# Receptance and value products of the second token group between the preparation steps of the first, and the second recurrence ahead of the first outputs

## The chip, the core and the metric

The kernel runs on one core of a Trainium2 chip. TensorE (PE in the rows) does the matrix products, VectorE (DVE) and ScalarE (ACT) the elementwise work, GpSimd (POOL) a smaller part of it, and SyncE (SP) issues the transfers. The metric is the time of one execution on the device in microseconds. The kernel before takes 2268.82 us (median of 3 runs, 2268.51 to 2272.32).

## The reference

One inference step of a decoder with two layers: layer 0 mixes tokens with an RWKV-7 recurrence, layer 1 with dilated attention, and each is followed by a gated feed-forward block. There are 512 prompt tokens and 8 x 4 = 32 sample tokens, 1024 features, 16 heads of 64. Only layer 0's mixing is touched. Cut to what matters:

```python
def rwkv7_time_mix(xn, x_last, S0, mu, w_rkv, ...):
    xs = xn[:, :, None, :] + xx[:, :, None, :] * mu
    rkv = jnp.einsum('btnc,ncd->btnd', xs[:, :, :3], w_rkv)
    r, k, v = rkv[:, :, 0], rkv[:, :, 1], rkv[:, :, 2]
    xw, xa, xg = xs[:, :, 3], xs[:, :, 4], xs[:, :, 5]
    w_log = -jax.nn.softplus(-(w0 + jnp.tanh(xw @ w1) @ w2)) - 0.5
    decay = jnp.exp(-jnp.exp(w_log.astype(F32)))
    a = jax.nn.sigmoid(a0 + (xa @ a1) @ a2)
    g = jax.nn.sigmoid(xg @ g1) @ g2
    ...
    y, S_T = wkv7_scan(rh, heads(decay), kh, vh, -kk, kk * ah, S0.astype(F32))
    ...
    bonus = jnp.sum(rh * kh * r_k, axis=-1, keepdims=True) * vh
    y = y + bonus.reshape(B, T, D)
    out = (y * g) @ w_o
```

The scan is `S = S * w_t + (S a_t) b_t + v_t k_t`, `y = S r_t` for each token and head.

## The kernel before

All products of the layer are float32 results of three passes over split operands (`mm3`, L98 to L100: high by high, high by low, low by high), where `split` (L74, L75) takes the high part on ScalarE and the low part on VectorE or GpSimd. The 544 token columns go in two groups, g0 with 288 (256 prompt and the 32 sample ones) and g1 with 256. A product of one kind (receptance i=0, key i=1, value i=2) for one group is 8 blocks m of 128 outputs, each 8 x 3 matmuls: 192 matmuls 128x288 or 128x256. `proj_gemm` runs it, loads its weights in transfers of 256 KB and splits them. Its inputs come from `mix`: 8 calls of `mix_block`, each one multiply-add on VectorE (`mix_t`, L306), one copy on ScalarE and one subtraction on VectorE or GpSimd. Tiles `mx` feed the three large products, `mxe` (one buffer) the low-rank ones of `lora1`.

The recurrence runs in chunks of 64 tokens. For each group, `prep(g)` calls `unit_prep` for 8 units of two heads: low-rank products L414 to L416, head sums L135, transposes of v (L458), elementwise work that ends in the tiles `AR`, `BK` and `BE`, and in a second half (after the `yield`) the bonus L485, the transposes of `BE` (L493) and the products of `BK` by `AR` (L498), which VectorE masks into `G`. The second half of a unit is issued after the first half of the next. `inverses` then solves the triangular systems of all chunks: copies of `G` into `X` (L515), a transpose (L518), 62 small VectorE operations (L523, L526), two transposes back (L529, L530), copies, and small products on TensorE (L539, L549). `chain`, which the text calls the scan, walks the chunks (from L570). `samples(hb)` does the sample tokens of half the heads (state loads and transposes L640, L648; products L653 to L706). `y_norm` takes mean and variance of the outputs (a power `y_var` on GpSimd, then four multiplications of `yt` there), and `y_out` applies gate and bonus and stores (`lg_hi`, `lg_lo`: split gate weights). `states` writes the final states. After the layer come `w_o`, the feed-forward blocks and attention.

The code is written as one stream, and the framework orders each engine's instructions from it; `Stream` (`c.slow`) limits how far the units of a preparation run ahead. Before, that gives: key and receptance for both groups with the low-rank products beside them; value for g0 with `prep(0)` in between, and value for g1 drawn into the same stretch; the rest of `prep(0)`; `inverses(0)`; scan(0); `samples(0)`, `prep(1)` and `samples(1)`; `inverses(1)`; scan(1) with `outputs(0)`; `states` and `outputs(1)`.

The lines of the driver that set this:

```python
        for m, _ in enumerate(proj_gemm(c, 2, mv, stage, groups=(0,))):
            next(p0, None)
        ...
        run(p0)
        inverses(c, st[0]["G"], sa)
        run(proj_gemm(c, 2, mv, stage, groups=(1,)))
        scan(0)
        ysm.append(samples(c, 0, smp[0], sp))
        run(prep(1))
        ysm.append(samples(c, 1, smp[1], sp))
        inverses(c, st[1]["G"], sa)
        outputs(0)
        scan(1)
```

Of the kernel before, what the change touches and what calls it, by code (L numbers as in the profile page):

```python
# [396 lines left out]
def unit_prep(c, g, m, b, up, un, G, UV):  # L397
# [11 lines left out]
    split(c, lhi, llo, lw, nc.vector, nc)  # L409
# [46 lines left out]
    ps = c.pp()  # L456
# [4 lines left out]
    BK = up.tile([128, 4, 2, 64], F, name="BK", bufs=c.ub)  # L461
# [4 lines left out]
    nc.vector.tensor_copy(c.dc[:, m, :, g], dp[:, :, 64])  # L466
# [38 lines left out]
def inverses(c, G, sp):  # L505
# [3 lines left out]
    nc = c.nc  # L509
    first, second = [[slice(side_of(par)[1].start + 32 * b, side_of(par)[1].start + 32 * b + 32) for par in range(2)]  # L510
# [3 lines left out]
    for r, view in blk:  # L514
        nc.scalar.activation(X[r], view, AF.Copy)  # L515
# [15 lines left out]
    for r, view in blk:  # L531
        nc.scalar.activation(view, X[r], AF.Copy)
    Z = sp.tile([128, 32, 32], F, name="XL", bufs=1)
    for n0 in (0, 16):
# [6 lines left out]
        for par in range(2):  # L541
            r1 = second[par]
            nc.scalar.activation(Z[r1, n0:n0 + 16, :], ps[par][r1, :].rearrange("p (n t) -> p n t", t=32), AF.Copy)
    for n0 in (0, 16):
# [6 lines left out]
        for par in range(2):  # L551
            r0 = first[par]
            nc.scalar.activation(G[r0, par, n0:n0 + 16, 96:128], ps[par][r0, :].rearrange("p (n t) -> p n t", t=32), AF.Copy)
# [181 lines left out]
def y_out(c, g, jj, yt, ys, yo):  # L735
# [13 lines left out]
    for par in range(2):  # L749
# [7 lines left out]
        split(c, lhi, llo, lg, nc.vector, nc)  # L757
# [25 lines left out]
def rwkv(c):  # L783
    nc, tc, a = c.nc, c.tc, c.a
    with ExitStack() as rx:
        ps = rx.enter_context(c.pool("ps", space=PSUM))
# [8 lines left out]
        c.pp = lambda: ps.tile([128, 512], F, name="pp", bufs=2)  # L795
# [26 lines left out]
        def scan(g):  # L822
            st[g]["yt"] = [sa.tile([128, 512], F, name=f"yt{x}", bufs=1) for x in range(4)]
            chain(c, g, st[g]["units"], st[g]["G"], st[g]["UV"], st[g]["yt"], sa)

        def outputs(g):
            y_norm(c, st[g]["yt"] + (ysm if g == 0 else []), yo)
# [15 lines left out]
        c.mm = lambda: pm.tile([128, 512], F, name="mm", bufs=6)  # L843
        stage = rp.enter_context(c.pool("stage", side="right"))
# [4 lines left out]
        with ExitStack() as ex:  # L849
# [15 lines left out]
            def side():  # L865
                for g in range(2):
                    mr.append(mix(c, 0, g, m1, "mx", bufs=2))
                    yield
                yield from lora1(c, lp, late, lambda i, g: mix(c, i, g, late, "mxe", bufs=1))
            sd = side()  # L870
            for _ in proj_gemm(c, 1, mk, stage):
                next(sd, None)
            for m, _ in enumerate(proj_gemm(c, 0, mr, stage)):
                next(sd, None)
                if m < 2:
                    mv.append(mix(c, 2, m, (ma, mb)[m], "mx", bufs=1))
            run(sd)
        rq.close()
        us = rx.enter_context(c.pool("us"))
        u0 = rx.enter_context(c.pool("u0"))  # L880
        up = rx.enter_context(c.pool("up"))
        c.ub = 1
        p0 = prep(0)
        for m, _ in enumerate(proj_gemm(c, 2, mv, stage, groups=(0,))):
            next(p0, None)
        px.close()
        ra.close()
        pm = py.enter_context(c.pool("ps_mm2", space=PSUM))
        c.mm = lambda: pm.tile([128, 512], F, name="mm", bufs=2)
        c.cw = lambda: pm.tile([128, 512], F, name="cw", bufs=1)  # L890
        c.cp = c.iv = lambda: pm.tile([128, 512], F, name="cp", bufs=3)
        run(p0)
        sa = rx.enter_context(c.pool("sa"))
        c.W = sa.tile([128, 512], F, name="W")
# [3 lines left out]
        inverses(c, st[0]["G"], sa)  # L898
        run(proj_gemm(c, 2, mv, stage, groups=(1,)))
        scan(0)  # L900
        py.close()
        rb.close()
        rp.close()
        pq = rx.enter_context(c.pool("ps_pp", space=PSUM))
        c.sm = lambda: pq.tile([128, 512], F, name="sm", bufs=1)
        c.cw = lambda: pq.tile([128, 512], F, name="cw", bufs=1)
        c.cp = c.iv = lambda: pq.tile([128, 512], F, name="cp", bufs=4)
# [738 lines left out]
```

## Time and profile before

| what | us |
|---|---|
| median of 3 runs | 2268.82 |
| lowest and highest | 2268.51, 2272.32 |
| the profiled execution | 2266.54 |
| its span, first to last instruction | 2264.80 |
| of the span, up to the end of the recurrent layer's recurrence | 604.20 |
| of the span, `w_o`, feed-forward, attention, feed-forward | 1660.60 |
| TensorE busy over the span | 2078.8 (92%) |
| mean granted TensorE clock, share of full speed | 0.937 |

Read the page first for the 40 slices: TensorE is full in all slices but some of the first eleven. Then cut these first 604 us into stages by the first instruction of each, and read busy time per engine and granted clock of every stage; the rows for that stand below.

### The profile page before, as it was taken

The numbers are of one execution on the slowest core, as the hardware profiler recorded it, in microseconds if no ns is written. First come the engines' busy times: TensorE is split into PE (matmuls) and PEld (weight loads), VectorE is DVE, ScalarE is ACT, GpSimd is POOL, SyncE is SP. The second block draws the span as 40 slices with busy tenths as digits, with TensorE's granted clock in tenths as the row PEclk, the third lists the DMA queues.
The fourth block names the chain that finished last, engine by engine and source line by source line (L and its number), as shares of the span: only waits on it lengthen the run. The fifth ranks groups of instructions, "written<-read, shape, count | busy, mean of one in ns | idle before, by whom it ended". The sixth has DMA issues, their size and how long they took to land. (4 is left out here: it accounts for less than half of the span.)

```text
span 2264.8 us, 48471 instructions
## 1 busy us (share of the span) xinstructions
PE 2078.8 (92%) x19286; PEld 1946.8 (86%) x19286; DVE 1167.0 (52%) x2454; ACT 896.4 (40%) x1847; POOL 552.1 (24%) x714
## 2 busy tenths in 40 slices
PE   7999647767599999999999999999999999999998
PEld 6998436546499999999989888888899799999998
DVE  7767565674574344325454454455444664444323
ACT  6555333323254444324333333333334454444323
POOL 5635513541232222102111111111111132222101
PEclk9999658668699999999999999999999999999999
DMA  5236201312653233335544444444444443232333
GB/s 162 91 119 195 74 19 32 74 22 67 175 148 91 83 90 93 93 100 168 138 134 133 120 128 127 119 126 139 123 133 122 133 132 93 85 94 85 88 89 108
DMA packets 435453, 245.96 MB, mean 109 GB/s; under 512 B 43194, under 2 KB 426330, under 8 KB 435098
## 3 DMA queue, kind: packets, MB, share of 16 engines
q1 hardware_dynamic: 435226, 242.86, 37.7%
q8 instruction: 152, 2.49, 0.4%
q14 instruction: 75, 0.61, 0.1%
HBM read 198.55 MB, written 30.85 MB: 101 GB/s over the span
## 5 line engine op out<-in xcount | busy, mean ns | idle before, releaser
L99 PE MATMUL mm<-xn,w_hi 128*128 128x256 f32 (+1 forms) x2688 | 788.0, 294 | 1.4 <-DVE xn L75 0.8
L98 PE MATMUL mm<-xn,w_hi 128*128 128x256 f32 (+1 forms) x2688 | 784.3, 293 | 3.6 <-ACT xn L984 3.6
L100 PE MATMUL mm<-xn,w_lo 128*128 128x256 f32 (+1 forms) x2688 | 780.1, 291 | 0.0
L75 DVE TENSOR_TENSOR w_lo<-w_raw,w_hi 128x512 fp32r<-128x512 f32 (+2 forms) x559 | 421.3, 756 | 568.2 <-ACT w_hi L74 557.2
L74 ACT ACTIVATE w_hi<-w_raw 128x512 fp32r<-128x512 f32 (+2 forms) x559 | 345.8, 620 | 542.1 <-PE mm L99 492.8
L98 PEld LDWEIGHTS mm<-xn,w_hi 128*128 128x128 f32 x2688 | 509.3, 190 | 10.1 <-ACT xn L984 4.2
L99 PEld LDWEIGHTS mm<-xn,w_hi 128*128 128x128 f32 x2688 | 509.6, 190 | 6.0 <-issue 2.8
L100 PEld LDWEIGHTS mm<-xn,w_lo 128*128 128x128 f32 x2688 | 508.8, 189 | 3.1 <-issue 3.0
L98 PE MATMUL mm<-act,w_hi 128*128 128x288 f32 (+1 forms) x704 | 200.4, 288 | 1.6 <-ACT y_out L1017 1.6
L99 PE MATMUL mm<-act,w_hi 128*128 128x288 f32 (+1 forms) x704 | 199.8, 288 | 0.0
L100 PE MATMUL mm<-act,w_lo 128*128 128x256 f32 (+1 forms) x704 | 198.7, 288 | 0.0
L1171 POOL TENSOR_TENSOR qk_raw<-qk_raw,rope 128x1088 f32<-128x1088 f32 x24 | 86.3, 3596 | 419.4 <-DMA qk_sw<-qk_raw 419.4
L98 PEld LDWEIGHTS mm<-act,w_hi 128*128 128x128 f32 x704 | 131.8, 189 | 1.7 <-ACT y_out L1017 1.7
L99 PEld LDWEIGHTS mm<-act,w_hi 128*128 128x128 f32 x704 | 131.6, 188 | 0.0
L100 PEld LDWEIGHTS mm<-act,w_lo 128*128 128x128 f32 x704 | 130.6, 188 | 0.0
L147 POOL TENSOR_TENSOR acc<-acc,sq_t 128x288 f32<-128x288 f32 (+1 forms) x56 | 46.7, 834 | 327.4 <-ACT sq_t L146 327.1
L98 PE MATMUL mm<-mx,w_hi 128*128 128x288 f32 (+1 forms) x384 | 112.1, 295 | 0.0
L100 PE MATMUL mm<-mx,w_lo 128*128 128x256 f32 (+1 forms) x384 | 110.3, 292 | 1.5 <-DVE w_lo L75 1.5
L99 PE MATMUL mm<-mx,w_hi 128*128 128x256 f32 (+1 forms) x384 | 111.2, 293 | 0.0
L1256 ACT ACTIVATE scores<-scores,sm_m 128x512 f32<-128x512 f32 (+3 forms) x80 | 50.4, 631 | 70.9 <-DVE sm_m L1255 68.9
L100 PEld LDWEIGHTS mm<-mx,w_lo 128*128 128x128 f32 x384 | 72.5, 190 | 2.4 <-DVE w_lo L75 2.1
L98 PEld LDWEIGHTS mm<-mx,w_hi 128*128 128x128 f32 x384 | 72.9, 191 | 1.1 <-ACT p_out L373 0.2
(360 smaller groups left out, 3287.0 us busy)
## 6 DMA issues: line engine op xcount, KB each, us to landing
w_raw<-ffn_w_up SPq DMA_DIRECT2D x176, 256.0 KB
w_raw<-attn_w_in SPq DMA_DIRECT2D x144, 256.0 KB
w_raw<-ffn_w_down SPq DMA_DIRECT2D x90, 256.0 KB
w_raw<-rwkv_w_rkv SPq DMA_DIRECT2D x64, 256.0 KB
qk_sw<-qk_raw SPq DMA_DIRECT2D x96, 136.0 KB
cache_k<-cache_k_w SPq DMA_DIRECT2D x96, 128.0 KB
cache_v<-cache_v_w SPq DMA_DIRECT2D x96, 128.0 KB
w_raw<-rwkv_w_o SPq DMA_DIRECT2D x32, 256.0 KB
```

The source lines that it names most:

```text
L74: (nc or c.nc).scalar.activation(out_hi, src, AF.Copy)
L75: lo_engine.tensor_tensor(out_lo, src, out_hi.bitcast(F), OP.subtract)
L98: nc.tensor.matmul(ps, hi, xhi(i), start=first and i == 0, stop=False)
L99: nc.tensor.matmul(ps, hi, xlo(i), start=False, stop=False)
L100: nc.tensor.matmul(ps, lo, xhi(i), start=False, stop=last and i == len(w) - 1)
L147: nc.gpsimd.tensor_tensor(acc, acc, t[:, :n], OP.add)
L1171: nc.gpsimd.tensor_tensor(raw, raw, c.rope[:, 0:1].to_broadcast([128, 2, NT]), OP.mult)
L1256: nc.scalar.activation(s[:, :w], s[:, :w], AF.Exp, scale=0.125, bias=m[:, 1:2], accum_out=m[:, 2:3])
```

## The change

- `mix`: all low parts are subtracted on GpSimd, not on VectorE and GpSimd in turn. `l_lo` and `lg_lo` go from VectorE to GpSimd, the copy into `dc` from VectorE to ScalarE.
- Receptance and value of g0 are computed ahead of `prep(0)`. Receptance and value of g1 (384 matmuls 128x256) come in two blocks m per unit of `prep(0)`; the receptance weights are loaded and split a second time for it.
- `BK` has two buffers in `prep(0)`, `pp` six PSUM buffers there and three later (two before); `yt` has two buffers, and `X` and its like lie in a pool of their own.
- The copies of `inverses` go to ScalarE and VectorE in turn, those into `X` in two halves.
- After scan(0) is issued, `prep(1)` goes one unit ahead, `samples(0)` stands before its next four units and `samples(1)` before the last; then `y_norm` of g0, `inverses(1)`, scan(1), `outputs(0)`, `states`, `y_norm` of g1 and `outputs(1)`.

```diff
@@ mix
-        mix_block(c, i, g, k, mx, c.nc.gpsimd if k % 2 else c.nc.vector)
+        mix_block(c, i, g, k, mx, c.nc.gpsimd)
@@ unit_prep
-    split(c, lhi, llo, lw, nc.vector, nc)
+    split(c, lhi, llo, lw, nc.gpsimd, nc)
...
-    BK = up.tile([128, 4, 2, 64], F, name="BK", bufs=c.ub)
+    BK = up.tile([128, 4, 2, 64], F, name="BK", bufs=c.ubk)
...
-    nc.vector.tensor_copy(c.dc[:, m, :, g], dp[:, :, 64])
+    nc.scalar.activation(c.dc[:, m, :, g], dp[:, :, 64], AF.Copy)
@@ inverses
+    def move(i):
+        return nc.vector.tensor_copy if i % 2 else lambda out, src: nc.scalar.activation(out, src, AF.Copy)
...
-    for r, view in blk:
-        nc.scalar.activation(X[r], view, AF.Copy)
+    by = lambda t: t.rearrange("p (c j) t -> p c j t", j=8)
+    for lo in (0, 4):
+        for i, (r, view) in enumerate(blk):
+            move(i)(by(X[r])[:, :, lo:lo + 4], by(view)[:, :, lo:lo + 4])
...
@@ y_out
-        split(c, lhi, llo, lg, nc.vector, nc)
+        split(c, lhi, llo, lg, nc.gpsimd, nc)
@@ rwkv
-            st[g]["yt"] = [sa.tile([128, 512], F, name=f"yt{x}", bufs=1) for x in range(4)]
+            st[g]["yt"] = [sa.tile([128, 512], F, name=f"yt{x}", bufs=2) for x in range(4)]
...
-            for m, _ in enumerate(proj_gemm(c, 0, mr, stage)):
+            for m, _ in enumerate(proj_gemm(c, 0, mr, stage, groups=(0,))):
                 next(sd, None)
...
+            for m, _ in enumerate(proj_gemm(c, 2, mv, stage, groups=(0,))):
+                if m == 1:
+                    mv.append(mix(c, 2, 1, mb, "mx", bufs=1))
...
-        c.cp = c.iv = lambda: pm.tile([128, 512], F, name="cp", bufs=3)
+        c.pp = c.iv = lambda: pm.tile([128, 512], F, name="pp", bufs=6)
+        p0 = prep(0)
+        rest = proj_gemm(c, 0, mr, stage, groups=(1,))
+        for m in range(9):
+            next(p0, None)
+            for _ in range(2):
+                next(rest, None)
+            if m == 4:
+                run(rest)
+                ra.close()
+                rest = proj_gemm(c, 2, mv, stage, groups=(1,))
         run(p0)
+        inverses(c, st[0]["G"], si)
+        run(rest)
...
-        ysm.append(samples(c, 0, smp[0], sp))
-        run(prep(1))
-        ysm.append(samples(c, 1, smp[1], sp))
-        inverses(c, st[1]["G"], sa)
+        scan(0)
+        p1 = prep(1)
+        next(p1)
+        for hb in range(2):
+            ysm.append(samples(c, hb, smp[hb], sp))
+            for _ in range(4):
+                next(p1)
+        run(p1)
+        y_norm(c, st[0]["yt"] + ysm, yo)
+        inverses(c, st[1]["G"], si)
+        scan(1)
         outputs(0)
-        scan(1)
         for hb in range(2):
             states(hb)
+        y_norm(c, st[1]["yt"], yo)
         outputs(1)
```

What the framework makes of it, at three places. On TensorE, one of the later units of `prep(0)` (`hwa` by `l_hi`: the low-rank products; `hr_e`: head sums; `in`: v), before:

```order
L498 MATMUL pp<-AR,BK 128x128 x8
L414 MATMUL pp<-hwa,l_hi 128x288
L415 MATMUL pp<-hwa,l_hi 128x288
L416 MATMUL pp<-hwa,l_lo 128x288
...
L135 MATMUL pp<-ca,hr_e 128x128 x3
L458 MATMUL pp<-ca,in_2926 64x128 x4
L485 MATMUL pp<-pb,ca 128x288
L493 MATMUL pp<-ca,BE 128x128 x4
L498 MATMUL pp<-AR,BK 128x128 x8
```

and an early unit of the changed kernel (`mx_1641`: mixed input of the receptance product of g1):

```order
L416 MATMUL pp<-hwa,l_lo 128x288
L100 MATMUL mm<-mx_1641,w_lo 128x256
L98 MATMUL mm<-mx_1641,w_hi 128x256
...
L135 MATMUL pp<-ca,hr_e 128x128 x3
L458 MATMUL pp<-ca,in_2659 64x128 x4
L98 MATMUL mm<-mx_1641,w_hi 128x256
...
L485 MATMUL pp<-pb,ca 128x288
L493 MATMUL pp<-ca,BE 128x128 x4
L498 MATMUL pp<-AR,BK 128x128 x8
```

Where a unit's own products followed each other, 28 matmuls of g1 now stand between L416 and L135, and 14 between L458 and L485; there are some 48 per unit, and none is left after the last unit's L498.

On GpSimd in the mixing stretch (`mxe`: inputs of the low-rank products; `rk`: powers for the norms of the keys), before:

```order
L383 TENSOR_TENSOR rk_81<-rs_k,mhalf 128x6
L75 TENSOR_TENSOR mxe_863<-mix_t,mxe_863 128x288 x3
L383 TENSOR_TENSOR rk_81<-rs_k,mhalf 128x4
L75 TENSOR_TENSOR mxe_863<-mix_t,mxe_863 128x288
L383 TENSOR_TENSOR rk_82<-rs_k,mhalf 128x6
```

and in the changed kernel:

```order
L75 TENSOR_TENSOR mxe_744<-mix_t,mxe_744 128x288 x8
L383 TENSOR_TENSOR rk_77<-rs_k,mhalf 128x6
L383 TENSOR_TENSOR rk_77<-rs_k,mhalf 128x4
L75 TENSOR_TENSOR mxe_889<-mix_t,mxe_889 128x288 x3
L383 TENSOR_TENSOR rk_78<-rs_k,mhalf 128x6
```

Of a mix of 8 blocks GpSimd took 4 and now takes 8, between the same powers.

On GpSimd at the end of `prep(1)` (`BK`, `BE`: the last unit; `y_var`: the power of the first group's `y_norm`), before:

```order
L59 TENSOR_TENSOR BK<-th_5072,di 128x4x64
L59 TENSOR_TENSOR BK<-tk,di 128x4x64
...
L59 TENSOR_TENSOR BE<-BK,dc 128x512
...
L59 TENSOR_TENSOR y_var<-y_var,mhalf 128x40
L59 TENSOR_TENSOR um<-Vs,cb 128x512
```

and in the changed kernel:

```order
L59 TENSOR_TENSOR BK<-th_5387,di 128x4x64
L59 TENSOR_TENSOR BK<-tk,di 128x4x64
L59 TENSOR_TENSOR y_var<-y_var,mhalf 128x40
L59 TENSOR_TENSOR BE<-BK,dc 128x512
L59 TENSOR_TENSOR um<-Vs,cb 128x512
```

The power now stands ahead of the last unit's `BE`, which L493 of that unit reads; L498 stands behind L493 on TensorE.

## Rows read from the trace of the kernel before

**Rows 1.** Stages: from:to us, length, busy of PE, PEld, DVE, ACT, POOL, clock, DMA, GB/s

```profile
32.60:165.90 133.30, 128.94 (x1001) 127.44 (x1000) 101.09 (x189) 75.72 (x188) 68.48 (x75) 0.97 0.38 118
165.90:233.60 67.70, 66.39 (x496) 61.70 (x494) 49.17 (x89) 36.63 (x81) 34.90 (x62) 1.00 0.63 185
233.60:294.30 60.70, 38.80 (x169) 28.99 (x167) 32.48 (x70) 18.67 (x40) 31.38 (x69) 0.58 0.25 69
294.30:338.40 44.10, 15.55 (x275) 13.28 (x275) 29.27 (x68) 13.46 (x21) 4.53 (x9) 0.50 0.01 4
338.40:370.60 32.20, 25.29 (x609) 23.63 (x608) 16.92 (x26) 8.41 (x16) 6.32 (x6) 0.89 0.01 2
370.60:465.10 94.50, 74.14 (x423) 58.54 (x420) 56.96 (x103) 37.00 (x77) 52.14 (x79) 0.75 0.28 66
465.10:518.20 53.10, 33.37 (x369) 24.46 (x369) 39.26 (x86) 14.41 (x21) 19.27 (x13) 0.57 0.13 22
518.20:563.00 44.80, 37.41 (x701) 32.30 (x699) 25.79 (x54) 10.15 (x23) 6.39 (x6) 0.91 0.22 64
563.00:604.20 41.20, 13.65 (x54) 9.42 (x49) 17.55 (x33) 7.24 (x16) 10.82 (x5) 0.56 0.60 175
604.20:2264.80 1660.60, 1626.95 (x15129) 1553.37 (x15129) 778.94 (x1693) 654.24 (x1319) 306.15 (x372) 0.99 0.41 115
```

**Rows 2.** TensorE's timeline: start, duration, line, tiles, of matmuls one behind the other

```profile
188.28 0.30 PE L99 MATMUL mm<-mx,w_hi 128*128 128x288 f32 x1
188.41 0.29 PE L100 MATMUL mm<-mx,w_lo 128*128 128x288 f32 x1
...
207.57 0.28 PE L99 MATMUL mm<-mx,w_hi 128*128 128x256 f32 x1
207.69 0.28 PE L100 MATMUL mm<-mx,w_lo 128*128 128x256 f32 x1
```

**Rows 3.** Groups by form, 32 to 168 us: total us, mean ns, idle before and releaser

```profile
L383 POOL TENSOR_TENSOR rk<-rs_k,mhalf 128x6 f32<-128x6 f32 x8 | 12.0, 1506 | 7.4 <-DVE rs_k L382 5.7 <-DMA w_raw<-rwkv_w_rkv 1.7
L75 POOL TENSOR_TENSOR mxe<-mix_t,mxe 128x288 fp32r<-128x288 f32 x12 | 10.7, 896 | 6.7 <-ACT mxe L74 6.7
L383 POOL TENSOR_TENSOR rk<-rs_k,mhalf 128x4 f32<-128x4 f32 x8 | 9.3, 1164 | 3.8 <-DVE rs_k L382 3.8
...
L75 DVE TENSOR_TENSOR w_lo<-w_raw,w_hi 128x512 fp32r<-128x512 f32 x32 | 23.0, 718 | 25.0 <-ACT w_hi L74 25.0
L75 DVE TENSOR_TENSOR mxe<-mix_t,mxe 128x288 fp32r<-128x288 f32 x12 | 6.0, 498 | 0.1
```

**Rows 4.** GpSimd's waits, 160 to 300 us: total us, times, longest

```profile
POOL BK L59 <- PE pp L498: 38.8, 7, 8.4
```

**Rows 5.** VectorE and TensorE timelines, first solve: its transposes, first product behind it

```profile
296.89 1.95 DVE L518 STREAM_TRANSPOSE XL<-X 128x1024 f32<-128x1024 f32 x1
...
323.13 1.91 DVE L529 STREAM_TRANSPOSE XT<-XL 128x1024 f32<-128x1024 f32 x1
...
325.10 0.32 PE L539 MATMUL cp<-XT,G 32*32 32x32 f32 x4 [22.80 <-DVE XT L529]
```

**Rows 6.** VectorE's timeline, second solve: the same two transposes

```profile
467.87 1.97 DVE L518 STREAM_TRANSPOSE XL<-X 128x1024 f32<-128x1024 f32 x1 [2.73 <-ACT X L515]
...
504.00 1.91 DVE L529 STREAM_TRANSPOSE XT<-XL 128x1024 f32<-128x1024 f32 x1
```

**Rows 7.** Timelines of SyncE and GpSimd: state loads of the samples, power of y_norm

```profile
372.93 2.90 SPq L640 DMA_DIRECT2D st<-state_rwkv_wkv  x4
...
489.08 7.78 POOL L59 TENSOR_TENSOR y_var<-y_var,mhalf 128x40 f32<-128x40 f32 x1 [5.63 <-DVE y_var L59]
```

**Rows 8.** Timelines of GpSimd and VectorE in the outputs of g1

```profile
572.79 5.39 POOL L59 TENSOR_TENSOR yt<-yt,y_var 128x512 f32<-128x512 f32 x4
...
573.33 5.40 DVE L75 TENSOR_TENSOR w_lo<-w_raw,w_hi 128x512 fp32r<-128x512 f32 x4 [6.19 <-ACT w_hi L74]
...
588.60 0.29 DVE L59 TENSOR_TENSOR lg_lo<-lg_raw,lg_hi 128x128 fp32r<-128x128 f32 x1 [0.51 <-ACT lg_hi L59]
```

More of the change, by code (lines that the diff above doesn't have):

```diff
@@ L530, in inverses @@
     nc.vector.transpose(X.rearrange("p n t -> p t n"), flat)
-    for r, view in blk:
-        nc.scalar.activation(view, X[r], AF.Copy)
+    for i, (r, view) in enumerate(blk):
+        move(i)(view, X[r])
     Z = sp.tile([128, 32, 32], F, name="XL", bufs=1)
@@ L542, in inverses @@
             r1 = second[par]
-            nc.scalar.activation(Z[r1, n0:n0 + 16, :], ps[par][r1, :].rearrange("p (n t) -> p n t", t=32), AF.Copy)
+            move(par)(Z[r1, n0:n0 + 16, :], ps[par][r1, :].rearrange("p (n t) -> p n t", t=32))
     for n0 in (0, 16):
@@ L552, in inverses @@
             r0 = first[par]
[L553 removed]
+            move(par)(G[r0, par, n0:n0 + 16, 96:128], ps[par][r0, :].rearrange("p (n t) -> p n t", t=32))
 def chain(c, g, units, G, UV, yt, sp):
@@ L843, in rwkv @@
         c.mm = lambda: pm.tile([128, 512], F, name="mm", bufs=6)
+        c.pp = lambda: pm.tile([128, 512], F, name="pp", bufs=2)
         stage = rp.enter_context(c.pool("stage", side="right"))
@@ L865, in side @@
             def side():
-                for g in range(2):
-                    mr.append(mix(c, 0, g, m1, "mx", bufs=2))
-                    yield
+                mr.append(mix(c, 0, 0, m1, "mx", bufs=2))
+                yield
                 yield from lora1(c, lp, late, lambda i, g: mix(c, i, g, late, "mxe", bufs=1))
             sd = side()
-            for _ in proj_gemm(c, 1, mk, stage):
+            for m, _ in enumerate(proj_gemm(c, 1, mk, stage)):
                 next(sd, None)
-            for m, _ in enumerate(proj_gemm(c, 0, mr, stage)):
+                if m == 5:
+                    mv.append(mix(c, 2, 0, m1, "mx", bufs=2))
@@ L879, in rwkv @@
         us = rx.enter_context(c.pool("us"))
         u0 = rx.enter_context(c.pool("u0"))
[L881 to L887, printed above, removed]
+        si = rx.enter_context(c.pool("si"))
+        ux = ExitStack()
+        up = ux.enter_context(c.pool("up"))
+        c.ub, c.ubk = 1, 2
         pm = py.enter_context(c.pool("ps_mm2", space=PSUM))
@@ L893, in rwkv @@
+        run(p0)
+        inverses(c, st[0]["G"], si)
+        run(rest)
+        py.close()
+        rb.close()
+        rp.close()
+        ux.close()
+        pq = rx.enter_context(c.pool("ps_pp", space=PSUM))
+        c.sm = lambda: pq.tile([128, 512], F, name="sm", bufs=1)
+        c.cw = lambda: pq.tile([128, 512], F, name="cw", bufs=1)
+        c.cp = lambda: pq.tile([128, 512], F, name="cp", bufs=3)
+        c.pp = c.iv = lambda: pq.tile([128, 512], F, name="pp", bufs=3)
         sa = rx.enter_context(c.pool("sa"))
+        up = rx.enter_context(c.pool("up1"))
@@ L894, in rwkv @@
+        c.ubk = 1
         c.W = sa.tile([128, 512], F, name="W")
```

19 lines of the change are left out of this document (3 added, 16 removed).

## The prediction

> **What bounds the kernel now.** I began with the 40 slices of the page and then cut the span into stages [rows 1]. The last stage, 1660.6 us from 604.20 on, has TensorE busy for 1626.95 us at a clock of 0.99, and the change leaves TensorE's work there alone: it counts as zero. Everything is decided in the first 604 us, where three kinds of stages alternate. While large products run, TensorE is the bound: busy 128.94 of 133.30 us and 66.39 of 67.70. Once the value products have run out, four of the eight units of `prep(0)` take 60.70 us at a granted clock of 0.58, with TensorE busy 38.80, VectorE 32.48 and GpSimd 31.38: no engine is full, and it is a chain from engine to engine that sets the pace. In the two solves (44.10 and 53.10 us at 0.50 and 0.57) the same holds, with VectorE's string of small operations as the chain. So the ground to win is the time in which TensorE idles or runs at half clock: 60.7, 44.1, 94.5, 53.1 and 41.2 us. The change moves products from stages where TensorE is full into the first of them.
>
> **Up to the first unit of `prep(0)`.** One matmul follows the next at 0.12 us with 256 columns and at 0.13 with 288 [rows 2]. Ahead of 165.9, receptance of g1 goes out (192 x 0.12 = 23.0) and value of g0 comes in (192 x 0.13 = 25.0): +1.9, so 168 at the least. To that comes the move of the low parts. By the last low-rank mix, 64 blocks (48 low-rank, 8 receptance, 8 value) lie on GpSimd, 32 more than before. On GpSimd one takes 896 ns, on VectorE 498 [rows 3]: GpSimd gains 32 x 0.896 = 28.7 us and VectorE loses 15.9. The powers of the key norms stay on GpSimd, 12.0 + 9.3 = 21.3 us, in the same queue. GpSimd then has 64 x 0.896 + 21.3 = 78.6 us of work, and with 0.56 us (6.7 / 12) of waiting for ScalarE before each block some 114, in a stage of 133.3. It fits, but no longer with room: the low-rank tile `mxe` has one buffer, so every delay goes on to the next mix, and TensorE has in front of it only what is left of receptance and value for g0. If the difference of 12.8 us all came through, the first unit would start at 181; if none, at 168. I take half: 174.
>
> The Trainium skill speaks against this move (GPSIMD Engine Reference, section 4.1, Engine selection): elementwise work with two inputs belongs on VectorE, since GpSimd is about twice as slow. The trace agrees nearly, 896 against 498 ns being 1.8 times; by the page's factor of 2 the difference would be an estimated 15.9 us and the upper end 184 in place of 181.
>
> **`prep(0)`.** Before, it lasted from 165.9 to 294.3. After, each unit carries 48 matmuls of g1, 5.8 us. What a unit needs of TensorE on its own: in the dense stretch 496 matmuls ran, 384 of them large, and these take 48 us of 67.7; the 112 others are those of four units, so 19.7 / 4 = 4.9 us each. TensorE's floor is thus 10.7 us per unit. GpSimd's is 31.38 / 4 = 7.8, and 8.3 with the two low parts that it now gets. The chain's is what ran before without large products: 60.70 / 4 = 15.2 us per unit. What sat in the chain was `BK`, which waited for the unit before's L498, 38.8 us in 7 waits, 5.5 us each [rows 4]; its second buffer takes that wait away. What is late next is `BE` with its one buffer, and TensorE's queue, in which a unit's L135, L485 and L493 now stand behind 14 to 28 matmuls (1.7 to 3.4 us). I expect 12 us per unit, nearer to TensorE's floor, since the gap between the two, 4.5 us, is less than the wait of 5.5 that goes; the clock should stay up, as in the dense stretch at 1.00. Seven units at 12 and 15 for the last with its second half: 174 + 84 + 15 = 273, **21 us less** than 294.3. The ends: 168 + 7 x 10.7 + 12 = 255 (39 less) and 181 + 7 x 15.2 + 15 = 302 (8 more). The second load of the receptance weights (16 transfers and splits) is hidden: DMA is busy at 0.25 and VectorE at 32.48 of 60.7 there.
>
> **`inverses(0)`.** The copies into `X` took from 294.3 to 296.9 on ScalarE alone; on two engines half, -1.3. The solve between the transposes, 296.89 to 325.04, stays but for some small operations of the preparation in between, -0.7. From L539 at 325.10 [rows 5] to the scan at 338.4 products and copies take turns for 13.3 us; the copies on two engines give -3 (0 to -5). Sum **-5** (-2 to -7).
>
> **scan(0)** took 32.20 us with TensorE busy 25.29. The first unit of `prep(1)` (4.9) and the first half of `samples(0)`, taken as much again, come into its queue: 10 us less what fits in the 6.9 idle ones. **+7** (3 to 11).
>
> **From scan(0) to scan(1)**, before 94.5 + 53.1 us. The unit that has gone into scan(0): an eighth of 94.5, -12. The rest of `samples(1)`, which ran beside the second solve from 465.1 until its power at 489.1, 24 us, now stands ahead of it; half beside the units, +12 (0 to 24). The power takes 7.78 us [rows 7] and stands on GpSimd ahead of the last unit's `BE`; behind it wait L493 and L498, `G`, `X` and the solve: +7.8. The 16 state loads of `samples(1)` are issued in a row into two buffers at 2.90 / 4 us each [rows 7], so 11.6 in all; TensorE's 16 transposes wait in order with the later units behind them: +8 (0 to 11.6). Against that, the second solve is free of the samples' work: between its transposes 467.87 to 505.91 [rows 6], 38.0 us, against 28.1 in the first [rows 5]: -9.9. The copies into `X` -1.4, those after the solve -2.5. Sum **+2** (-18 to +18).
>
> **scan(1) with outputs(0)**, 44.80 us against 32.20 for the scan alone. The outputs are still needed in between, but the scan goes first: I take 3 of the 12.6, **-3** (-8 to +2). **`states`, `y_norm` and outputs of g1**, 41.20 us: eight `lg_lo` go from VectorE, 0.29 each, to GpSimd at some 0.5, behind the multiplications of `yt` (5.39 us) [rows 8]: **+3** (0 to 8).
>
> **The sum.** -21 - 5 + 7 + 2 - 3 + 3 = -17 on the profiled execution's 2266.5, which is 2249.5. That execution lies 2.3 us under the median of 2268.8, so 2252 for the median.
>
> **The rivals.** First, **the units keep their 15.2 us**. The wait on `BK` may only have hidden another, `BE`'s or that for TensorE's queue, so that the chain is as long as before: 174 + 7 x 15.2 + 15 = 295, 22 us later than in the sum, which gives 2274; with the mixes late as well (181) 2281. It decides from about 15 us per unit on. For it speaks that 60.7 us held no full engine, and that at the half clock the 48 matmuls would take 11.6 in place of 5.8 us; against it the 5.5 us that go. What would feed it: beside the four `yt` multiplications, four `w_lo` took 5.40 us on VectorE, 1.35 each [rows 8], against 0.718 [rows 3], so the two engines hold each other up where they work at once. The Trainium skill gives the reason (SBUF — State Buffer, section SBUF: two separate sides): VectorE with two inputs from there and GpSimd share one pair of ports, which one of them holds for a whole instruction. By that rule the low parts moved to GpSimd would still stop VectorE, the chain would be no shorter, and the time would be that of this rival.
>
> Second, **the power and `samples(1)` go ahead of the second solve in full**: nothing of their 24 us lies beside units, and the loads show all 11.6 us. That is +15.6: 2268. For it: the order of GpSimd; against it: in the 94.5 us of `prep(1)` TensorE is idle for 20.
>
> Third, **more is hidden**: units at TensorE's floor (7 x 1.3 = -9) and the samples' 12 us beside the units: 2231. That the change doesn't do what it says is excluded, since the order has the products of g1 between the units' own.
>
> **How the numbers follow.** Forecast 2252, 0.42; units as before 2274 to 2281, 0.25; samples in front of the solve 2268, 0.20; more hidden 2231, 0.13. About 0.2% is what a measurement of this kernel can tell from no change: 2264.3 to 2273.4. Faster: 0.42, 0.13 and a third of the second rival, 0.62. Slower: nearly all of the first rival, 0.23. Within: 0.15. The range takes in the forecast's open terms, the second rival and the nearer part of the other two: 2232 to 2277.
>
> **What would show it.** In the profile after, the first L135 of `prep(0)` at about 174; L135 of successive units about 12 us apart, with the clock over 0.9 until 270; the first transpose of `X` at about 275 and 28 us to the one back; the first L539 of the second solve right behind a VectorE string without other work; the power `y_var` 128x40 on GpSimd just before the last `BE`. I am wrong if units stay at 15 us or the clock drops to half among them, if the low-rank mixes are TensorE's last wait before 180, or if the stretch from scan(0) to scan(1) grows by more than 15.

## The result and the profile after

The changed kernel takes 2258.43 us (median of 4 runs, 2257.57 to 2258.71) against 2268.76 for the kernel before on the same chip: a ratio of 0.995, 95% interval 0.9933 to 0.9967. The forecast was 2252. The profiled execution's span is 2255.50, 9.3 us less than before's 2264.80; the forecast sum was 17 less.

The same cut into stages as in [rows 1], for the kernel after (columns as there). The first row ends with the first unit's L135, the second with the last masked `G` of `prep(0)`; then follow the first solve, scan(0), the rest up to the last `G` of `prep(1)`, the second solve, scan(1), the outputs of g1, and all behind:

```profile
139.80:193.40 53.60, 49.27 (x347) 46.28 (x346) 33.59 (x47) 29.18 (x63) 19.09 (x24) 1.00 0.62 182
193.40:283.00 89.60, 77.68 (x659) 70.56 (x658) 77.74 (x143) 53.72 (x128) 76.31 (x138) 0.98 0.59 170
283.00:318.80 35.80, 7.26 (x258) 7.02 (x258) 30.34 (x72) 4.35 (x6) 0.20 (x1) 0.52 0.14 39
318.80:358.80 40.00, 35.78 (x716) 31.61 (x716) 24.07 (x39) 17.10 (x37) 19.42 (x28) 0.96 0.09 22
358.80:467.50 108.70, 83.09 (x424) 62.15 (x424) 62.31 (x101) 35.59 (x77) 65.17 (x86) 0.67 0.26 58
467.50:505.80 38.30, 12.57 (x276) 11.80 (x276) 30.93 (x74) 4.36 (x6) 0.51 (x2) 0.52 0.07 12
505.80:548.40 42.60, 36.87 (x698) 33.00 (x696) 24.42 (x48) 11.02 (x24) 10.02 (x13) 0.87 0.23 68
548.40:593.20 44.80, 14.30 (x49) 10.18 (x49) 12.97 (x25) 6.87 (x15) 13.51 (x13) 0.53 0.55 161
593.20:2255.50 1662.30, 1625.11 (x15129) 1552.77 (x15129) 778.29 (x1693) 654.20 (x1319) 305.99 (x372) 0.99 0.41 115
```

Set against the stages of before, step by step:

| step | before | after | difference | forecast |
|---|---|---|---|---|
| up to the last `G` of `prep(0)` | 294.3 | 283.0 | -11.3 | -21 |
| first solve, to scan(0) | 44.1 | 35.8 | -8.3 | -5 |
| scan(0) | 32.2 | 40.0 | +7.8 | +7 |
| rest of `prep(1)` with the samples | 94.5 | 108.7 | +14.2 | together +2 |
| second solve | 53.1 | 38.3 | -14.8 | |
| scan(1) with outputs(0) | 44.8 | 42.6 | -2.2 | -3 |
| `states`, outputs of g1 | 41.2 | 44.8 | +3.6 | +3 |
| all behind | 1660.6 | 1662.3 | +1.7 | 0 |

Every step but the first lies within 3.5 us of its forecast. In the first, two large differences stand against each other. TensorE's timeline gives the start of the units: L135 of the first, the fifth and the last unit of `prep(0)` in the kernel before, then of the first and the last in the changed kernel:

```profile
169.34 0.38 PE L135 MATMUL pp<-ca,hr_e 128*128 128x128 f32 x2
...
235.76 0.33 PE L135 MATMUL pp<-ca,hr_e 128*128 128x128 f32 x1 [0.55 <-ACT th L59]
...
272.93 0.33 PE L135 MATMUL pp<-ca,hr_e 128*128 128x128 f32 x1
```
```profile
193.45 0.33 PE L135 MATMUL pp<-ca,hr_e 128*128 128x128 f32 x1
...
270.77 0.33 PE L135 MATMUL pp<-ca,hr_e 128*128 128x128 f32 x1
```

The units begin at 193.4, where 174 was forecast, at most 181, and where they began at 169.3 before. But then seven steps take 77.3 us, 11.0 each, where 12 was forecast; before, L135 of the first and the last unit lay 103.6 us apart, 14.8 each: 16.6 each up to the fifth unit, beside the large products, and 12.4 each for the three steps behind them, without large products. The rest of the last unit, up to the last `G`, takes 12.2 us. The wait of `BK` on L498 [rows 4] is no longer among GpSimd's waits in this stretch.

So the question is what made the start so late. GpSimd's timeline, from the first block of a low-rank mix to the last one, and TensorE's longest wait among them:

```profile
60.98 1.02 POOL L75 TENSOR_TENSOR mxe<-mix_t,mxe 128x288 fp32r<-128x288 f32 x1
...
112.03 6.36 POOL L75 TENSOR_TENSOR mx<-mix_t,mx 128x288 fp32r<-128x288 f32 x7
118.34 7.05 POOL L75 TENSOR_TENSOR mxe<-mix_t,mxe 128x256 fp32r<-128x256 f32 x8
...
138.10 0.76 POOL L75 TENSOR_TENSOR mxe<-mix_t,mxe 128x256 fp32r<-128x256 f32 x1
```

```profile
118.23 0.58 PE L98 MATMUL mm<-mxe,lw_hi 128*128 128x256 f32 x1 [8.20 <-ACT mxe L74]
```

Between 61 and 139 GpSimd is busy for 66.6 of 77.9 us; the two rows below cover that stretch and the key mixes ahead of it. And the eight blocks of the value mix (`mx`, 110.1 to 118.4, the last seven of them in the row above) stand ahead of the low-rank mix that TensorE waits 8.20 us for.

```profile
32.60:90.00 57.40, 51.47 (x379) 50.93 (x378) 44.22 (x67) 34.93 (x88) 49.00 (x49) 0.91 0.37 124
90.00:139.80 49.80, 38.80 (x287) 38.24 (x287) 35.67 (x55) 25.02 (x62) 41.11 (x44) 0.86 0.21 63
```

### The profile page after: what moved, and what is told of

Its sections match the earlier page's. It is cut to its first block, busy times and chain, and to the rows that moved or that the text cites. A ratio compares the mean times of both kernels' runs of the same rounds, so it can differ in the third digit from the quotient of the medians.

```text
span 2255.5 us, 48553 instructions
## 1 busy us (share of the span) xinstructions
PE 2049.3 (91%) x19286; PEld 1926.7 (85%) x19286; DVE 1173.4 (52%) x2402; ACT 895.2 (40%) x1867; POOL 612.4 (27%) x786
## 5 line engine op out<-in xcount | busy, mean ns | idle before, releaser
L75 DVE TENSOR_TENSOR w_lo<-w_raw,w_hi 128x512 fp32r<-128x512 f32 (+1 forms) x575 | 434.7, 758 | 561.9 <-ACT w_hi L74 550.8
L74 ACT ACTIVATE w_hi<-w_raw 128x512 fp32r<-128x512 f32 (+1 forms) x575 | 355.8, 620 | 551.1 <-PE mm L99 488.7
L100 PE MATMUL mm<-mx,w_lo 128*128 128x288 f32 (+1 forms) x384 | 114.3, 300 | 3.4 <-DVE w_lo L75 3.3
L98 PE MATMUL mm<-mx,w_hi 128*128 128x288 f32 (+1 forms) x384 | 114.1, 299 | 1.7 <-ACT w_hi L74 1.6
L99 PE MATMUL mm<-mx,w_hi 128*128 128x288 f32 (+1 forms) x384 | 113.5, 297 | 0.0
```

Of the source, the lines that this page charges most:

```text
L74: (nc or c.nc).scalar.activation(out_hi, src, AF.Copy)
L75: lo_engine.tensor_tensor(out_lo, src, out_hi.bitcast(F), OP.subtract)
L98: nc.tensor.matmul(ps, hi, xhi(i), start=first and i == 0, stop=False)
L99: nc.tensor.matmul(ps, hi, xlo(i), start=False, stop=False)
L100: nc.tensor.matmul(ps, lo, xhi(i), start=False, stop=last and i == len(w) - 1)
```

## The experiments

On the chips of these runs executions of one kernel spread over 6 to 20 us, and in the profiles the stages behind the output projection, which no experiment touches, differ by 14 us (last section). So two things are read from each: the ratio with its interval, and the stages of its profile up to the output projection, of which the changed kernel's repetition (below) agrees within 1 us at the first L135 and within 4 us at the projection; a difference between two profiles that is no larger than that is not told from none.

Behind scan(0) there is a second caution: an edit far ahead changes the order that the framework makes there. GpSimd's power stands ahead of the last unit's `BE` in the changed kernel, in its repetition and with the outputs first; ahead of its `BK` as well with the mixes in turn and with both mends; and behind `BE` with one `BK` buffer, with the products ahead, with the value mix late and with the copies on ScalarE, though none of these touches it. What those runs show of their own edit is read up to scan(0).

Line numbers from L515 on stand five further down in the changed kernel: the first transpose of `X`, L518 before, is L523. Of the first and the second solve it stands at

```profile
284.01 1.90 DVE L523 STREAM_TRANSPOSE XL<-X 128x1024 f32<-128x1024 f32 x1
...
469.36 1.93 DVE L523 STREAM_TRANSPOSE XL<-X 128x1024 f32<-128x1024 f32 x1
```

### The low parts of the mixes in turn

```diff
-        mix_block(c, i, g, k, mx, c.nc.gpsimd)
+        mix_block(c, i, g, k, mx, c.nc.gpsimd if k % 2 else c.nc.vector)
```

> The changed kernel with one edit undone: in the mixes, the low parts are subtracted on GpSimd and VectorE in turn again. Theory A (the mixes on GpSimd are what makes the first unit of prep(0) start at 193.4 us in place of the 174 forecast): the first L135 comes at 178 to 182, GpSimd's busy time between 60 and 120 us falls from 52.6 to about 35, and the time falls by 11 to 15 us, to 2243 to 2247. Theory B (the new order of the products sets the start: receptance and value of the first group with the wider blocks, 339 matmuls behind the last low-rank product): the first L135 stays at 190 or later and the time within 3 us of 2258.

Ratio 0.9948 (0.9933 to 0.9964). The first L135 of `prep(0)`, from TensorE's timeline:

```profile
180.94 0.33 PE L135 MATMUL pp<-ca,hr_e 128*128 128x128 f32 x1
```

12.5 us earlier, as theory A had it. But the time hardly moved. The first transpose of `X` comes at 278.59 in place of 284.01, so 7.1 of the 12.5 are gone by the end of `prep(0)`, one of whose units took 19.3 us; and the output projection starts at 589.11 in place of 593.16, hardly more than two profiles of one kernel differ by. The cause of the late start is shown; that it is worth its whole length, 11 to 15 us, was wrong.

### Only the mixes on GpSimd, in the kernel before

The same line the other way round, in the kernel before.

> The kernel before with only this part of the change: all low parts of the mixes on GpSimd. Theory A: the first L135 moves from 169.3 to 177 to 183 and the time goes up by 8 to 14 us, to 2277 to 2283. Theory B: the mixes still fit beside the products, the first L135 stays within 2 us of 169.3 and the time within 3 us of 2268.8.

Ratio 1.0076 (1.0058 to 1.0094): slower, by more than either end. TensorE's timeline has

```profile
182.80 0.27 PE L135 MATMUL pp<-ca,hr_e 128*128 128x128 f32 x1
```

13.5 us behind the 169.3 of before, and here nothing is given back: scan(0) starts 13.0 us later, the output projection 16.7. In this kernel the edit is a loss by itself.

### One buffer for BK

```diff
-        c.ub, c.ubk = 1, 2
+        c.ub, c.ubk = 1, 1
```

> The changed kernel with one BK buffer in prep(0) in place of two. Theory C (the second buffer took the wait on L498 out of the unit's chain, as the prediction said): units go from 11.1 to 13.5 to 15 us, so 17 to 27 us more, 2275 to 2285. Theory D (the products of the second group in between, with TensorE at full clock, are what shortened the units; BK's wait had room): units stay within 0.7 us of 11.1 and the time within 5 us of 2258.

Ratio 1.0025 (1.0011 to 1.0039), against 0.995 with two. GpSimd's waits from 193 to 300 us have the old wait again, and the first transpose of `X` comes 15.8 us later:

```profile
POOL BK L59 <- PE pp L498: 22.4, 7, 6.1
```
```profile
299.85 1.90 DVE L523 STREAM_TRANSPOSE XL<-X 128x1024 f32<-128x1024 f32 x1
```

Seven unit steps take 87.5 us, 12.5 each, less than the 13.5 that theory C asked for, and the last unit's tail 19.4 in place of 13.2. So the wait was in the chain, as theory C says; its size per unit was too large. It is not the whole of the gain either: from the first L135 to this transpose it was 127.6 us before, is 90.6 in the changed kernel and 106.9 with one buffer, so 16.4 of 37.0 us come back.

### The products of the second group ahead of the units

```diff
-        for m in range(9):
-            next(p0, None)
-            for _ in range(2):
-                next(rest, None)
...
+        run(proj_gemm(c, 0, mr, stage, groups=(1,)))
+        ra.close()
+        rest = proj_gemm(c, 2, mv, stage, groups=(1,))
+        run(rest)
         run(p0)
```

> The changed kernel with the receptance and value products of the second group ahead of prep(0) and not between its units; the order then still draws three units into them, and five stand alone. Theory C (two BK buffers shorten the unit's chain by themselves): the five units alone take 10.5 to 12 us each, the first transpose of X comes at 290 to 300. Theory D (the products keep TensorE at full clock and that is what shortens the units): the five take 14 to 16 each, the first transpose of X at 308 to 320, 22 to 34 us later than the 284 to 286 of the changed kernel, ratio 1.005 to 1.011.

Ratio 1.0066 (1.0044 to 1.0089). The stretch of four of the units that stand alone (windows, columns as above), and the first transpose of `X`:

```profile
258.30:299.00 40.70, 22.62 (x141) 17.60 (x141) 28.43 (x58) 16.73 (x43) 31.59 (x66) 0.66 0.35 94
```
```profile
312.57 1.90 DVE L523 STREAM_TRANSPOSE XL<-X 128x1024 f32<-128x1024 f32 x1
```

10.2 us per unit with TensorE's clock at 0.66, where the three steps without large products took 12.4 before: full clock is not needed for the short unit, which speaks against theory D's reason. GpSimd no longer waits for L498 in this stretch. That the second `BK` buffer alone does it, as theory C says, is not shown: `prep(0)` also has six `pp` buffers in PSUM here in place of two, and `l_lo` and the copy into `dc` on other engines; no run takes these apart. With 48 products in it a unit took 11.0, so 5.8 us of products cost 0.8 per unit. The transpose at 312.57 and the ratio are what theory D had expected (308 to 320, 1.005 to 1.011), and not C's 290 to 300, but for another reason than D's: not long units, but most of the products' 46 us in front of the units that stand alone. Having them between the units is worth 28.6 us here.

### Samples placed as before

```diff
-        p1 = prep(1)
-        next(p1)
-        for hb in range(2):
-            ysm.append(samples(c, hb, smp[hb], sp))
-            for _ in range(4):
-                next(p1)
-        run(p1)
+        ysm.append(samples(c, 0, smp[0], sp))
+        run(prep(1))
+        ysm.append(samples(c, 1, smp[1], sp))
```

> The changed kernel with samples(0) issued ahead of the whole of prep(1) and samples(1) behind it, as before; in the order GpSimd's power then stands behind the last unit's BE. Theory E (the power and the rest of samples(1) in front of the last unit cost nearly what the clean second solve gains, +2 in the sum): the second solve takes 34 to 38 us in place of 25.9, the last G comes 8 to 14 us earlier, and the time is within 4 us of 2258. Theory F (the power and the block of state loads are a net loss): 6 to 16 us less, 2242 to 2252.

Ratio 0.9975 (0.996 to 0.9991), an interval that touches the changed kernel's. The first transpose of the second `X` comes at 454.86 (469.36 in the changed kernel), that is 14.5 us earlier, and the solve up to the transpose back takes 37.1 us in place of 25.9. From scan(0) to scan(1) it is 182.4 in place of 187.0. Theory E was nearer: the two nearly cancel, with some 5 us for the old place by the profile (6 against the repetition below), which the times don't show.

### The changed kernel again, the value mix late, both mends, the copies

Four kernels on one chip. First the changed kernel as it is:

> The changed kernel as it is, run beside the three others on the same chip, so that they can be set against it directly: a ratio of 0.993 to 0.997 to the kernel before, the first L135 of prep(0) at 192 to 195 us and the first matmul of the output projection at 592 to 595.

Ratio 0.9978 (0.9959 to 0.9997), a smaller gain on this chip, though the intervals overlap, with L135 at 192.5 and the output projection at 596.7: ratio and projection a little above what was expected.

```diff
-                if m == 5:
+                if m == 7:
                     mv.append(mix(c, 2, 0, m1, "mx", bufs=2))
```

> The changed kernel with the value mix of the first group issued two blocks of the key product later, behind the last low-rank mix in place of ahead of it; nothing else. Theory A (GpSimd's queue of mixes sets the start, and the 8 value blocks at 0.9 us that stand ahead of the last low-rank mixes are part of it): the last low-rank product ends at 130 to 133 in place of 139.7, TensorE's wait of 8.2 us for a mix goes, and the first L135 comes 6 to 9 us earlier, 185 to 187. Theory B (a wait for the weights of the value product follows anyway): the first L135 at 191 or later.

Ratio 0.9932 (0.991 to 0.9955). The wait of 8.20 us is gone, the last low-rank product ends at 133 and L135 stands at

```profile
189.04 0.33 PE L135 MATMUL pp<-ca,hr_e 128*128 128x128 f32 x1
```

3.5 us earlier than in the run beside it, not 6 to 9: theory A in sign, about half in size. It is clear of chance: the six profiles whose start was left alone have it at 191.6 to 194.2. scan(0) starts 2.4 us earlier and the output projection 4.0; the second solve starts 14.9 us earlier, since the order behind scan(0) changed too and the power stands behind `BE`, but from scan(0) to the projection it is 274.2 us against 275.7. The medians differ by 9.2 us, more than the profiles, and how much of that is the value mix is open.

> The value mix late and the low parts on GpSimd and VectorE in turn. Theory A: both delays add, the last low-rank product ends at 119 to 123 and the first L135 comes at 169 to 175. Of the gain in the start, theory G (the loads that feed the units, 1 MB of weights each, give back about half, as in the run with the mixes in turn alone) keeps 9 to 12 us at the first transpose of X, 272 to 275; theory H (that one long unit was chance) keeps 18 to 24, 260 to 266. Time 2240 to 2252 on the scale of the first runs.

Ratio 0.994 (0.9919 to 0.9962), which on the scale of the first runs is 2255 and not 2240 to 2252. The last low-rank product ends at 124.2 and not by 123, the start is at 173.5, and the first transpose of `X` 15.8 us earlier than in the run beside it, better than theory G and short of H:

```profile
173.49 0.33 PE L135 MATMUL pp<-ca,hr_e 128*128 128x128 f32 x1
```
```profile
270.36 1.90 DVE L523 STREAM_TRANSPOSE XL<-X 128x1024 f32<-128x1024 f32 x1
```

But scan(1) starts only 8.5 us earlier: from scan(0) to the first transpose of the second `X` it takes 159.4 us, against 152.0 beside it and 150.6 in the first profile of the changed kernel. The timelines of GpSimd and TensorE in the changed kernel, up to the last unit's `BE` and L493 (L702 and L706, L697 and L701 before: the state updates of `samples(1)` and the transposes that bring them out):

```profile
453.67 6.77 POOL L59 TENSOR_TENSOR y_var<-y_var,mhalf 128x40 f32<-128x40 f32 x1
460.42 1.03 POOL L59 TENSOR_TENSOR BE<-BK,dc 128x512 f32<-128x512 f32 x1
```
```profile
462.47 1.12 PE L706 MATMUL sm<-ca,Ss 128*128 128x128 f32 x4 [0.79 <-DVE Ss L59]
463.38 1.06 PE L493 MATMUL pp<-ca,BE 128*128 128x128 f32 x4
```

and with both mends, with VectorE's transpose behind them:

```profile
440.00 6.78 POOL L59 TENSOR_TENSOR y_var<-y_var,mhalf 128x40 f32<-128x40 f32 x1 [3.86 <-DVE y_var L59]
446.75 0.73 POOL L59 TENSOR_TENSOR BK<-th,di 128x256 f32<-128x256 f32 x1
447.45 0.73 POOL L59 TENSOR_TENSOR BK<-tk,di 128x256 f32<-128x256 f32 x1
448.14 1.04 POOL L59 TENSOR_TENSOR um<-Vs,cb 128x512 f32<-128x512 f32 x1
449.14 3.03 POOL L59 TENSOR_TENSOR yt<-yt,y_var 128x512 f32<-128x512 f32 x3
452.14 1.04 POOL L59 TENSOR_TENSOR BE<-BK,dc 128x512 f32<-128x512 f32 x1
```
```profile
458.16 1.12 PE L706 MATMUL sm<-ca,Ss 128*128 128x128 f32 x4 [0.78 <-DVE Ss L59]
459.07 1.06 PE L493 MATMUL pp<-ca,BE 128*128 128x128 f32 x4
```
```profile
464.57 1.91 DVE L523 STREAM_TRANSPOSE XL<-X 128x1024 f32<-128x1024 f32 x1
```

The second solve starts 24.6 us after the power, against 15.7 in the changed kernel, 8.9 us more. Two orders make that up. On GpSimd the power and three multiplications of `yt` now stand ahead of `BE`, and the power ahead of `BK` too: `BE` ends 13.2 us after the power's start in place of 7.8. On TensorE L493 stands behind the fourth of the state updates in place of the third: it starts 5.9 us after `BE` has ended, in place of 1.9. GpSimd's order alone doesn't lose the time: with the mixes in turn alone it is the same, L493 stands behind the third update, 1.2 us after `BE`, and the second solve starts 150.2 us after scan(0), as in the changed kernel. This is the mechanism of the prediction's second rival, power and samples ahead of the second solve, but not its size: from scan(0) to scan(1) it takes 195.8 us, 16.0 more than the 179.8 of before, where the rival had 24.6 more.

All copies of `inverses` on ScalarE:

```diff
     def move(i):
-        return nc.vector.tensor_copy if i % 2 else lambda out, src: nc.scalar.activation(out, src, AF.Copy)
+        return lambda out, src: nc.scalar.activation(out, src, AF.Copy)
```

> The changed kernel with all copies of inverses on ScalarE, as before, still in two halves. The prediction's term was 5 us for the first solve and 3.9 for the second: from the last G to the first transpose 1 to 2 us more, from the transpose back to the scan 12 to 13.5 us in place of 9, in both solves, so 8 to 10 us more in all. Rival (VectorE's copies only take the place of ScalarE's and the products in between set the pace): within 2 us.

Ratio 0.9986 (0.9968 to 1.0004), not to be told from 0.9978. In the profile the way from the transpose back to the scan is 13.1 us in place of 9.0 in the first solve and 13.3 in place of 10.5 in the second, as expected; from the last `G` to the first transpose it is 0.4 us more in the first solve, not 1 to 2. scan(0) starts 5.6 us later, 4.5 of them in the solve, and the output projection 7.5. The medians differ by 1.8 us, which is the rival's figure, and the intervals allow some -4 to +8: the term's mechanism is in the trace, its size in the time was not resolved.

### The mended start with the samples as before, and with the whole second half as before

Both mends (mixes in turn, value mix late) and, for the first kernel, the samples' edit from above; for the second also `inverses(1)` ahead of `y_norm`, `outputs(0)` ahead of scan(1) and the PSUM buffers of before.

> Both mends of the start (low parts of the mixes in turn, value mix late) and the samples placed as in the kernel before. From the profiles so far: first L135 at 173 to 175, scan(0) at 304 to 307, from there to the output projection 270 as with the samples placed as before (against 274 to 282 in the order of the change), so the output projection at 574 to 578, 18 us earlier than the changed kernel's 593 to 597: ratio 0.987 to 0.991 to the kernel before. Rival (the gain in the start is given back behind scan(0) whatever the order, as in the run with both mends): the output projection at 585 or later, ratio 0.993 to 0.996.

> The same, with the whole second half in the order and with the PSUM buffers of the kernel before (cp four, pp two; outputs(0) ahead of scan(1)). In the kernel before it took 265.8 us from scan(0) to the output projection, less 3.9 for the copies on two engines in the second solve: output projection at 567 to 573, ratio 0.985 to 0.989, if the second half's new order is the net loss that the profiles show. Rival (the old order was as fast only with the old start, since two units of prep(1) had begun in the first solve): as z1 or slower, 576 or later.

Ratios 0.9886 (0.9863 to 0.9909) with a median of 2245.23, and 0.9878 (0.9851 to 0.9904) with 2242.97: both faster than either kernel, and not to be told from each other. In the first the second solve no longer waits for the power, which stands behind `BE` again: GpSimd's power came at 457.8, and the transpose of `X` 18.2 us ahead of it. The output projections, of the first and of the second kernel:

```profile
574.71 0.61 PE L98 MATMUL mm<-y,w_hi 128*128 128x288 f32 x1 [4.32 <-ACT y L74]
```
```profile
580.19 0.61 PE L98 MATMUL mm<-y,w_hi 128*128 128x288 f32 x1 [4.38 <-ACT y L74]
```

The first is where it was expected, 18.5 us ahead of the changed kernel's; the second, expected at 567 to 573, is not, and stands where its rival had it (576 or later). From scan(0) to the projection the first takes 272.0 us and the second 274.6, where the old order took 265.8 in the kernel before: its two units of `prep(1)` that run ahead of scan(0) there stand behind it here. So the second half's new order as a whole is not the net loss that I had read into it. What shows is the place of the samples: with the mended start 272.0 us with the samples as before against 282.3 in their new place; without it 270.0 against 274.4 and 275.7, a difference that is hardly more than two profiles of one kernel show. Since the framework's order changes with each of these edits, that the power's place is the cause is argued and not shown.

### Outputs ahead of the second recurrence

```diff
-        scan(1)
         outputs(0)
+        scan(1)
```

> The changed kernel with one thing undone: outputs(0) issued ahead of scan(1). The prediction's term for it was 3 us, the profiles show 2 (44.6 to 42.6 us from the first to the last step of scan(1)). Theory: scan(1) takes 44 to 47 us and the output projection starts 0 to 4 us later than 593 to 597; ratio 0.995 to 0.999. Rival (the recurrence ahead is worth its whole difference to a bare scan, 12 us): 603 or later.

Ratio 1.0003 (0.9985 to 1.0021), 0.3 to 0.5% above the changed kernel's two ratios, where 0 to 4 us were expected. In the profile scan(1) takes 43.1 us in place of 42.6, less than the 44 to 47 expected, and the output projection starts at

```profile
600.77 0.61 PE L98 MATMUL mm<-y,w_hi 128*128 128x288 f32 x1 [4.25 <-ACT y L74]
```

which is 4.0 to 7.6 us later; of these about 2 to 4 had arisen before scan(0). From scan(0) on it is 277.7 us against 274.4 and 275.7: 2 to 3 us for the recurrence ahead of the outputs, about what the two profiles of the changed kernel differ by. The times say more, 6 to 12 us, but across chips and with intervals that allow 0 to 18. The whole 12 of the rival are not in the profile; the times don't exclude them.

## Why the prediction was right, and where it was off

**The direction and the range** held: faster, -0.5%, where -0.74% was forecast. The stage up to the last `G` of `prep(0)` owes part of that to luck: against the 273 of the sum the units start 19.4 us late, their seven steps are 6.7 us shorter and the last unit's rest 2.8, which leaves 10.

**Up to the first unit: the step that failed.** The change's one large loss lies here. The prediction had 78.6 us of low-rank and value mixes and powers on GpSimd, set them against the whole stage of 133.3 us, found that they fit, and passed on half of the 12.8 us by which GpSimd gets slower than VectorE. The amount was about right: from the first low-rank mix to the last, 61.0 to 138.9, GpSimd has 66.6 us of it, and the waits in between make that 77.9. The stage was wrong. The first low-rank mix starts at 61 and not at 32.6, since the key mixes and the first receptance mix are ahead of it, so GpSimd was not occupied for 78.6 of 133 us but all the time until the last product that needs it. Mixes in turn brought 12.5 us back and the same edit alone in the kernel before cost 13.5, so all of the difference came through. The second part was not in the sum at all: the value mix, moved ahead of the last two low-rank mixes, stands in the same queue (3.5 us alone). With both undone the first L135 is at 173.5. That this is near the 174 forecast is chance: without the moves the prediction's own figure is 168, counted from 165.9, the first value matmul, and not from L135 at 169.3. From L135 to L135 TensorE then starts its units 4.2 us later than before, where the products alone were put at 1.9.

The Trainium skill had spoken against this edit (GPSIMD Engine Reference, section 4.1, Engine selection), and the runs agree: a 128x288 block takes 963 ns on GpSimd in the changed kernel, against 498 on VectorE [rows 3], and the edit delays the first unit in both kernels; that it costs time is shown in the kernel before alone.

```profile
L75 POOL TENSOR_TENSOR mxe<-mix_t,mxe 128x288 fp32r<-128x288 f32 x24 | 22.5, 963 | 2.0 <-ACT mxe L74 2.0
```

**`prep(0)`** went 12 forecast, 11.0 measured per unit, near TensorE's floor of 10.7. The reason given, the wait on `BK`, was right in part: one buffer brings back 15.8 us at the solve, but 1.5 us per unit and not 5.5; the rest of the gain was not taken apart. The chain's 15.2 us was mis-sized: it is a quarter of 60.7 us, which hold the whole rest of the last unit, some 21 us, while the steps without large products took 12.4. That the clock would stay up was right: 0.98. The first rival, units at 15.2, is out. The Trainium skill describes the shared ports that were to feed it (SBUF — State Buffer, section SBUF: two separate sides). Whether such holds occurred is not plain from the trace: against the units alone of before, `AR<-kk,dx` on VectorE took 778 ns in place of 446 and `th<-kk,th` on GpSimd 1154 in place of 853, but `cl<-scan,th` on VectorE 771 in place of 1379. They did not keep the units at 15: in the stretch of the unit steps TensorE was busy 70.25 of 77.40 us, VectorE 67.28 and GpSimd 65.85, and these shares don't tell work from being held up.

```profile
193.40:270.80 77.40, 70.25 (x596) 64.72 (x595) 67.28 (x124) 47.32 (x113) 65.85 (x119) 0.98 0.63 183
```

**The solves and scans** came out at -8.3 for -5, +7.8 for +7, -2.2 for -3. The first lies outside its own range of -2 to -7: between the transposes the solve lost 2.4 us where 0.7 was put, and behind them 4.4 where 3 was put. **From scan(0) to scan(1)** the sum of +2 was -0.6: `prep(1)` with the samples grew by 14.2 where its parts made +15.8, the second solve shrank by 14.8 (13.8). The single parts of the 15.8 were not taken apart. The 16 state loads of `samples(1)` did take 10.96 us in a row, as put:

```profile
402.15 10.96 SPq L645 DMA_DIRECT2D st<-state_rwkv_wkv  x16
```

One argument in it was poor: that a unit moves from here into scan(0). In the kernel before, two units of `prep(1)` had run L135 by 301.6, in the first solve, so it had that credit already.

**The second rival** (power and samples ahead of the second solve in full) didn't show in the changed kernel, whose stage came out at -0.6; the power does stand ahead of `BE` there and holds it up for its 6.8 us, where the sum had 7.8. With both mends part of the rival shows. What stays open is why 7 us of an earlier start were lost within `prep(0)` with the mixes in turn alone and 3 with both mends; the loads of weights were named for it and not tested.

## What to carry to other kernels

Weigh work that is moved to a slower engine against the time from the first to the last piece that someone waits for, not against the stage around it. An earlier stage is worth its length only if the next order is unchanged: after an edit read the queue orders again, of every engine on the chain, since a generated order can put a long operation in front of a short one that holds up a chain. Here a second buffer on the tile that closes a chain from engine to engine was worth more (15.8 us at the solve) than either move between engines (12.5 to 13.5 us lost by the mixes, 5.6 gained at scan(0) by the copies).

## What the runs showed of the hardware

The stages behind the output projection hold the same 15,129 TensorE instructions in every kernel, and yet took from 1658.7 to 1672.6 us in the profiles. In the changed kernel (row at the top) and in the kernel before with the mixes on GpSimd the order of them on TensorE is the same, and they differ by 9.3 us, with GpSimd, ScalarE and VectorE busy for the same time and TensorE for 6.5 us more:

```profile
620.90:2292.50 1671.60, 1631.60 (x15129) 1558.71 (x15129) 778.97 (x1693) 653.78 (x1319) 306.26 (x372) 0.99 0.40 114
```

Most of the difference is TensorE's clock. The first 457 us of these stages take the same time in both; of the rest, up to shortly before the end, the changed kernel and then the other one:

```profile
1050.00:2250.00 1200.00, 1170.84 (x11544) 1099.73 (x11544) 572.49 (x1302) 460.64 (x970) 213.81 (x221) 0.99 0.42 117
```
```profile
1078.00:2287.50 1209.50, 1177.08 (x11544) 1105.92 (x11544) 573.45 (x1303) 461.17 (x971) 214.21 (x221) 0.98 0.41 117
```

The granted clock falls from full to half in places where TensorE has waited: in the changed kernel it was busy for 1.74 of the 4.70 us ahead of 1052.7, and then the clock stood at 0.51. The time at half clock in these two rows comes to 20 us in the changed kernel and 37 in the other; 17 us more at half the clock are an estimated 8.5 us of work at the full one. Over all fourteen profiles the time behind the projection goes with the time at half clock in it: 20 us of it in the shortest (1658.7), 48 in the longest (1672.6). Why TensorE waits oftener in one execution than in another is not shown.

That is as much as the whole change moved, so for such a change the stages of the profile said more than one time did.
